# Squares of the residual placed later on ScalarE in the last stage of a hybrid encoder block

## The chip, the cores and the metric

One core of a Trainium2 chip runs the kernel. The metric is device time in microseconds of one execution, from the same chip for the kernel before and after; lower is better. TensorE (PE in the profile) multiplies matrices into PSUM, VectorE (DVE) and ScalarE (ACT) do elementwise work, GpSimd (POOL) does little here but issue DMAs that add to what lies in memory, SyncE (SP) issues the other DMAs. Each engine works through one queue in order, so an operation that waits holds all that stand behind it.

## The reference

256 rows of width 4096, everything in float32. After a norm, one wide product feeds chunked attention and a convolution module; their gated results go through `w_out` and are added to `x`. The last stage, which the change is about, is this:

```
h = h + jnp.concatenate([y_a, y_c], axis=-1) @ w_out[i]
gate = jax.nn.sigmoid(rms_norm(h, ple_norm_g[i]) @ w_ple_gate[i] + b_ple_gate[i])
h = h + gate * (p[i] @ w_ple[i])
return rms_norm(h, final_g)
```

So every row needs the sum of squares of the final h over all 4096 columns, and each element is multiplied by `final_g` and by the row's inverse root.

## The kernel before, in words

**Precision and tiling.** A float32 product is made of three matmuls on float32r parts: the high part of the weights `wh` (a cast on ScalarE) and the low part `wl` (weights minus `wh`, a subtraction on VectorE), both in `parts_of`, line 204 and 205. The activations, transposed and split once, lie in SBUF; the weights stream through. A product is made for a pair of column blocks of 512 at a time (`mixed_product`). Its 32 row blocks of 128 form 16 units of two. A *plain* unit is 24 matmuls of 512 columns. A *seven* unit (marked `*`, `+` or `-` in the orders) uses Strassen's seven products and needs 21, for which VectorE first forms four sums of weight blocks, `ua` and `ub` (lines 518 to 532); they are cast and subtracted like weights, as `uh` and `ul`. Units marked `+` have `ua` formed by DMAs that add, and use it only in the products from `w_in`.

**Buffers.** Loaded weights `wt` have five, `wh` and `wl` three each, `uh` and `ul` two, `ua` and `ub` two between them. The seven units' extra products P1, P5, P7, P6 take the four PSUM banks of the pool `ps_tmp`, which the embedding product `pacc` of the column pair before has held. Rows broadcast over partitions (bias of the gate, `final_g`) share three buffers.

**The last stage.** `gated_pair` runs for the column pairs 0, 2 and 4 (pairs 1, 2 and 3 in the text); the last pair has its own code, with the order `final` in place of `dense`. In a gated pair, 16 units of `w_ple_gate` are followed by the embedding product from `w_ple` (line 237). Then, for each quarter of the pair's 256 x 1024 block, the gate is finished on VectorE (line 1269) and put through a sigmoid on ScalarE (line 1270). What is left is not issued at once but put in a list, `later`: the gate times the embedding on VectorE (into `z`, which frees a bank of `pacc`), a DMA on POOL's queue that adds `z` to the residual `hc` (written in line 1272, L184 in the profile), eight empty places, the squares of `hc` with their row sums on ScalarE (line 610, output `junk`), and `hc` times `final_g` on VectorE. Helpers such as `tt` have one line for all their uses, so the profile shows those two multiplies as L184, told apart by their tiles: `z<-acc,z` and `hc<-hc,row`.

**The order.** `mixed_product` of the next pair calls `fill(4)` after each unit, which writes four entries of the list: the multiplies and their DMAs in units 0 and 1, eight empty places in units 2 and 3, the squares in unit 4, the weight multiplies in unit 5, the loads of two bias rows (appended when the first seven unit begins) in unit 6. That is program order only. A planner then orders every engine's queue by simulating the program with its own costs: an operation takes its engine when its inputs are there by that simulation, so one can be issued long before its place in the program if its engine is idle. `tc.issue_after(ins)` gives all that is written within it on `ins`'s engine an edge: they are queued behind `ins`, without a wait.

`recent` holds what `parts_of` made last. Units marked `+` use it (`queued_behind`): the cast and the subtraction of `ua` are queued behind those of the weights before them.

The orders that matter, the number being the pair of row blocks:

```
dense = units("1 0* 3 2* 5 4* 6* 7 8* 9 10* 11 12* 14* 13 15")
final = units("1 0* 3 2* 5 4* 6* 7 8* 9 10* 12* 11 13 14 15")
```

Unit 0 is thus the plain "1", unit 1 the seven "0*", unit 6 "6*".

Of the kernel before, what the change touches and what calls it, by code (L numbers as in the profile page):

```python
# [25 lines left out]
def hybrid_block(  # L26
# [153 lines left out]
    later = deque()  # L180
# [6 lines left out]
    def weight_parts(w, col, k0, kc, tiles=None):  # L187

        wt = wpool.tile([P, KC, NB], F32, tag="w", name="wt")
        nc.sync.dma_start(  # L190
            wt[:, :kc, :],
            w[k0 * P : (k0 + kc) * P, col : col + NB].rearrange("(k q) n -> q k n", q=P),
        )
        return parts_of(wt, kc, tiles)[0]

    def part_tiles():
        return [wpool.tile([P, KC, NB], F32R, tag=tag, name=tag, bufs=3) for tag in ("wh", "wl")]

    def parts_of(wt, kc, tiles=None):
        if tiles is None:  # L200
            tiles = part_tiles()
        wh, wl = tiles
        made = (
            nc.scalar.copy(wh[:, :kc, :], wt[:, :kc, :]),  # L204
            nc.vector.tensor_tensor(  # L205
                wl[:, :kc, :], wt[:, :kc, :], wh[:, :kc, :].bitcast(F32), ALU.subtract
            ),
        )
        recent[:] = made
        return (wh, wl), made  # L210

    def high_and_minus(wt):
# [7 lines left out]
    recent = []  # L220

    @contextmanager
    def queued_behind(made):

        with ExitStack() as queued:
            for ins in made:
                queued.enter_context(tc.issue_after(ins.ins))
            yield

    def accumulate(acc, h, lhs, kb, wh, wl, k, kblocks, then=lambda ins: None):  # L230
        t, i = lhs[kb // 4], kb % 4
        xh = t[:, i, 0, h * P : (h + 1) * P]
        xl = t[:, i, 1, h * P : (h + 1) * P]
        for kind in range(3):
            a, b = ((xh, wh), (xl, wh), (xh, wl))[kind]
            then(
                nc.tensor.matmul(  # L237
                    acc, a, b[:, k, :],
                    start=kb == 0 and kind == 0, stop=kb == kblocks - 1 and kind == 2,
                )  # L240
            )

    def product(w, col, lhs, kblocks, pool=None, tag="acc", fills=2):

        acc = [
            (pool or ps_acc).tile([P, NB], F32, tag=tag, name=f"acc{h}") for h in range(NH)
        ]
        for k0 in range(0, kblocks, KC):
            kc = min(KC, kblocks - k0)
            wh, wl = weight_parts(w, col, k0, kc)  # L250
            for k in range(kc):
                for h in range(NH):
                    accumulate(acc[h], h, lhs, k0 + k, wh, wl, k, kblocks)
            fill(fills)
        return acc
# [79 lines left out]
    def pair_parts(src):  # L335

        tiles = [upool.tile([P, 2, NB], F32R, tag=tag, name=tag) for tag in ("uh", "ul")]
        return parts_of(src, 2, tiles)[0]
# [38 lines left out]
    def mixed_product(  # L377
# [93 lines left out]
        for n, (pair, seven, by_dma) in enumerate(order):  # L471
# [13 lines left out]
            if n >= len(order) - n_left:  # L485
                for k in range(2):
                    tiles = left[2 * (n - len(order) + n_left) + k]
                    held.append((2 * pair + k, parts_of(wts[k], 2, tiles and tiles())[0]))
                fill(fills[n % len(fills)])
                continue  # L490
# [29 lines left out]
            with queued_behind(before if seven == "+" else ()):  # L520
                uah, ual = pair_parts(ua)
# [50 lines left out]
    def helper_sums(helper, z):  # L572


        nc.scalar.copy(z[1][0], helper["P1"])
        tt(z[1][0], helper["P6"], z[1][0], ALU.add)
        tt(z[0][1], helper["P5"], z[1][0], ALU.add)
        tt(z[1][0], helper["P7"], z[1][0], ALU.add)
        tt(z[1][1], helper["P5"], z[1][0], ALU.add)

    def sum_tiles(*homes):

        homes = homes or (dict(tag="stage"),) * 2
        t = [spool.tile([P, NH, NB], F32, name="z", **kw) for kw in homes]
        return t, [[t[j][:, h] for j in range(2)] for h in range(NH)]
# [481 lines left out]
    def broadcast_row(src, n0, n, **kw):  # L1067

        kw = kw or dict(tag="row", bufs=3)
        t = spool.tile([P, n], F32, name="row", **kw)  # L1070
        nc.sync.dma_start(
            t, bass.AP(tensor=src.tensor, offset=src.offset + n0, ap=[[0, P], [1, n]])
        )
        return t
# [122 lines left out]
    for c0 in range(0, D // NB, 2):  # L1197
        for j in range(2):
            hc = act.tile([P, NH, NB], F32, tag="act", name="hc")
# [20 lines left out]
        for h, j in QUARTERS:  # L1220
            hc = hs[c0 + j][:, h, :]
# [10 lines left out]
    ssq_f = cpool.tile([P, NH, n_f + 2], F32, name="ssq_f")  # L1232
    nc.vector.memset(ssq_f[:, :, :1], EPS)
    square_f = partial(square_sum, scale=D ** -0.5)
# [4 lines left out]
    def gated_pair(c0, order, ahead):  # L1239

        z, rows, fgs = [], [], []

        def on_begin():
            later.extend(partial(bias_row, rows, c0 + j) for j in range(2))

        def on_helpers(helper):
            z.extend(sum_tiles()[1])
            stt(z[0][0], helper["P1"], r_h[:, :1], rows[0], ALU.mult, ALU.add)
            helper_sums(helper, z)
            for h, j in QUARTERS[1:]:  # L1250
                zz = z[h][j]
                stt(
                    zz, zz, r_h[:, h : h + 1], rows[j],
                    ALU.mult, ALU.subtract if j else ALU.add,
                )
            fgs.extend(broadcast_row(final_g, (c0 + j) * NB, NB) for j in range(2))

        acc = mixed_product(
            w_ple_gate[0], c0 * NB, hT, hS, order, on_helpers, ahead=ahead, fills=(4,),
            on_begin=on_begin,  # L1260
        )
        pacc = [
            product(w_ple[0], (c0 + j) * NB, pT, PLE // P, pool=ps_tmp, tag="tmp", fills=0)
            for j in range(2)
        ]
        squares, weights = [], []
        for h, j in QUARTERS:
            gt, hc = z[h][j], hs[c0 + j][:, h, :]
            stt(gt, acc[h][j], r_h[:, h : h + 1], gt, ALU.mult, ALU.subtract if j else ALU.add)
            nc.scalar.activation(gt, gt, AF.Sigmoid)  # L1270
            later.append(partial(tt, gt, pacc[j][h], gt, ALU.mult))
            later.append(partial(nc.gpsimd.dma_start, hc, gt, accum_op=ALU.add))
            squares.append(partial(square_f, ssq_f[:, h, 1 + c0 + j : 2 + c0 + j], hc))
            weights.append(partial(tt, hc, hc, fgs[j], ALU.mult))
        later.extend([lambda: None] * 8 + squares + weights)

    for c0 in range(0, n_f - 2, 2):
        gated_pair(c0, dense if c0 else late, None if c0 else h_ahead)


    c0 = n_f - 2
# [100 lines left out]
    squares = []  # L1382
# [45 lines left out]
```

## Time and profile before

| | |
|---|---|
| median of 3 runs | 2049.0 us (2047.79 to 2050.46) |
| the profiled execution | 2048.76 us |
| its span, first to last instruction | 2047.0 us |
| TensorE busy | 98% |
| VectorE busy | 94% |
| ScalarE busy | 61% |
| granted TensorE clock, mean | 0.998 |
| the last stage, with the products of `w_ple_gate` | from about 1650 us on |

The profile shows one execution. Its span leaves out 1.76 us at the ends. A timeline row gives start, length, engine, line, operation, what it writes and reads, and in brackets how long the engine had been idle and what ended that. A matmul's length overlaps with that of the next, so the pace is read from a stretch: its time by its matmuls. A table by stretches gives the span of each, then busy time and instructions of PE, weight loads (PEld), DVE, ACT and POOL, the granted clock, the DMA share and GB/s.

### The profile page before, as it was taken

Reading aid. Unit: us, or ns where it says so; the run is one execution under the profiler, and the core shown is the slowest. Engines: PE = TensorE matmul, PEld = TensorE weight load, DVE = VectorE, ACT = ScalarE, POOL = GpSimd, SP = SyncE. Lnnn points to the kernel's source line nnn. Section 1 sums busy time; section 2 is a strip of 40 time slices with the busy share of each in tenths; the row PEclk is TensorE's granted clock in tenths of the full one; section 3 lists DMA queues with packets and bytes.
Section 4 is the critical chain, followed back from the end, with each engine's and each line's share of the span. In section 5 each row is a group of like instructions: output and inputs, shape, how many; then the busy total and the mean of one; then the engine's idle time right before and its main releaser. Section 6 shows DMA issues by size and latency. Waiting matters only on the chain. (4 is left out here: it accounts for less than half of the span.)

```text
span 2047.0 us, 26349 instructions
## 1 busy us (share of the span) xinstructions
PE 2009.9 (98%) x9043; PEld 1648.4 (81%) x9043; DVE 1922.0 (94%) x2759; ACT 1258.1 (61%) x1634; POOL 75.8 (4%) x83
## 2 busy tenths in 40 slices
PE   9999999999999999999999999999999999898987
PEld 7888888878888888888888788888888888686866
DVE  7999999889999998989999999999999999898997
ACT  7655455664656556775666566766676665555554
POOL 0000000000000000000000000000000000000000
PEclk9999999999999999999999999999999999999999
DMA  8787878679678877556678677776876856766665
GB/s 288 224 238 233 257 212 251 176 229 256 183 214 256 242 211 224 179 177 205 211 218 250 202 236 222 223 248 201 237 227 219 246 172 222 206 217 206 216 209 170
DMA packets 175921, 450.86 MB, mean 220 GB/s; under 512 B 14494, under 2 KB 17710, under 8 KB 175786
## 3 DMA queue, kind: packets, MB, share of 16 engines
q1 hardware_dynamic: 161952, 417.93, 63.5%
q0 software_dynamic: 13184, 30.41, 8.7%
q8 instruction: 71, 1.16, 0.2%
q10 hardware_dynamic: 650, 0.84, 0.1%
q14 instruction: 64, 0.52, 0.1%
HBM read 441.78 MB, written 4.19 MB: 218 GB/s over the span
## 5 line engine op out<-in xcount | busy, mean ns | idle before, releaser
L420 PE MATMUL acc<-wh,big_t 128*128 128x512 f32 x4028 | 1240.7, 391 | 1.6 <-DVE z L1138 1.6
L204 ACT CAST wh<-wt 128x1024 fp32r<-128x1024 f32 (+1 forms) x716 | 684.1, 965 | 480.8 <-PE acc L420 349.1
L420 PEld LDWEIGHTS acc<-wh,big_t 128*128 128x128 f32 x4028 | 753.6, 188 | 158.0 <-issue 1.7
L205 DVE TENSOR_TENSOR wl<-wt,wh 128x1024 fp32r<-128x1024 f32 (+1 forms) x716 | 791.6, 1117 | 43.2 <-ACT wh L204 37.1
L420 PE MATMUL acc<-wl,big_t 128*128 128x512 f32 x1958 | 759.9, 392 | 0.1
L420 PEld LDWEIGHTS acc<-wl,big_t 128*128 128x128 f32 x1958 | 367.4, 188 | 77.2 <-DVE wl L205 1.2
L204 ACT CAST uh<-ua 128x1024 fp32r<-128x1024 f32 x187 | 196.5, 1051 | 101.8 <-DVE ua L519 50.0
L205 DVE TENSOR_TENSOR ul<-ua,uh 128x1024 fp32r<-128x1024 f32 x187 | 228.9, 1224 | 13.1 <-ACT uh L204 10.3
L787 DVE SCALAR_TENSOR_TENSOR cv<-uT,dw,cv 128x255 f32<-128x255 f32 (+23 forms) x480 | 206.8, 478 | 1.1
L420 PE MATMUL acc_P<-uh,big_t 128*128 128x512 f32 x570 | 176.7, 392 | 11.8 <-DVE z L184 6.9
L420 PEld LDWEIGHTS acc_P<-uh,big_t 128*128 128x128 f32 x570 | 105.7, 188 | 38.7 <-DVE z L184 8.1
L204 ACT CAST uh<-ub 128x1024 fp32r<-128x1024 f32 x99 | 104.1, 1052 | 50.1 <-DVE ub L532 41.1
L205 DVE TENSOR_TENSOR ul<-ub,uh 128x1024 fp32r<-128x1024 f32 x99 | 120.8, 1221 | 3.5 <-ACT uh L204 3.1
L420 PE MATMUL acc_P<-ul,big_t 128*128 128x512 f32 x285 | 111.5, 393 | 7.0 <-DVE ul L205 7.0
L518 DVE TENSOR_TENSOR ua<-wt 128x512 f32<-128x512 f32 x112 | 77.0, 687 | 14.6 <-DMA wt<-in_w_in_dram 8.7
L420 PE MATMUL acc<-uh,big_t 128*128 128x512 f32 x286 | 88.3, 389 | 0.0
L420 PE MATMUL acc_P<-wh,big_t 128*128 128x512 f32 x286 | 88.2, 389 | 0.0
L519 DVE TENSOR_TENSOR ua<-wt 128x512 f32<-128x512 f32 x112 | 76.9, 687 | 3.8 <-DMA wt<-in_w_in_dram 3.0
L420 PEld LDWEIGHTS acc_P<-ul,big_t 128*128 128x128 f32 x285 | 53.3, 188 | 22.3 <-DVE ul L205 11.3
L420 PE MATMUL acc_P<-uh,comb_t 128*128 128x512 f32 x228 | 70.2, 390 | 0.3 <-ACT uh L204 0.3
L532 DVE TENSOR_TENSOR ub<-ub,wt 128x512 f32<-128x512 f32 x99 | 68.2, 689 | 1.6
L531 DVE TENSOR_TENSOR ub<-ua,wt 128x512 f32<-128x512 f32 x99 | 67.9, 686 | 0.0
(254 smaller groups left out, 1637.7 us busy)
## 6 DMA issues: line engine op xcount, KB each, us to landing
wt<-in_w_in_dram SPq DMA_DIRECT2D x416, 512.0 KB, 4.7
wt<-in_w_out_dram SPq DMA_DIRECT2D x128, 512.0 KB, 4.5
wt<-in_w_ple_gate_dram SPq DMA_DIRECT2D x128, 512.0 KB, 4.2
wt<-in_w_pw_dram SPq DMA_DIRECT2D x32, 512.0 KB, 4.5
ua<-in_w_in_dram SPq DMA_DIRECT2D x31, 512.0 KB, 4.6
ua<-in_w_in_dram POOLq DMA_DIRECT2D x31, 512.0 KB, 8.5
wt<-in_w_in_dram SPq DMA_DIRECT2D x31, 256.0 KB, 2.7
low<-in_w_in_dram POOLq DMA_DIRECT2D x12, 512.0 KB, 8.8
```

Source lines behind the costliest of these rows:

```text
L204: nc.scalar.copy(wh[:, :kc, :], wt[:, :kc, :]),
L205: nc.vector.tensor_tensor(wl[:, :kc, :], wt[:, :kc, :], wh[:, :kc, :].bitcast(F32), ALU.subtract),
L420: nc.tensor.matmul(banks[name], a, b, start=name not in begun, stop=final and ends[name] == n and kind == 2 and not (left and name in "P2 ...
L518: plus(ua[:, 0], w0[:, 0], w0[:, 1])
L519: plus(ua[:, 1], w0[:, 1], w1[:, 1])
L531: plus(ub[:, 0], ua[:, 0], w1[:, 1])
L532: plus(ub[:, 1], ub[:, 0], w1[:, 0])
L787: nc.vector.scalar_tensor_tensor(cv[:, i, PAD - k :], uT[:, i, : T + k - PAD], dw[:, b, k : k + 1], cv[:, i, PAD - k :], ALU.mult, ALU.add,)
```

## The change

The squares of a gated pair are written eight empty places later: sixteen in place of eight, so in unit 6 of the next product, the weight multiplies in unit 7 and the bias rows in unit 8. And each square is queued on ScalarE behind the cast that `parts_of` wrote last before it. For that, `recent` keeps the cast alone (`made[:1]`) in place of cast and subtraction, in all products.

```
         recent[:] = made
+        recent[:] = made[:1]
         return (wh, wl), made
...
+    recent = []
+
+    def behind_cast(work, *args):
+
+        with tc.issue_after(recent[0].ins):
+            return work(*args)
...
-            squares.append(partial(square_f, ssq_f[:, h, 1 + c0 + j : 2 + c0 + j], hc))
+            squares.append(partial(behind_cast, square_f, ssq_f[:, h, 1 + c0 + j : 2 + c0 + j], hc))
             weights.append(partial(tt, hc, hc, fgs[j], ALU.mult))
-        later.extend([lambda: None] * 8 + squares + weights)
+        later.extend([lambda: None] * 16 + squares + weights)
```

The second `recent = []` binds the same name anew before anything uses it. `gated_pair` runs three times; the squares of its last run fall into the last pair's product.

## The prediction

> **What bounds the kernel now.** I read the page's busy times first, then a table of busy time by stretch, then the waits of the last stage, then its timeline engine by engine.
>
> ```profile
> span 2047.0 us, 26349 instructions
> PE 2009.9 (98%) x9043; PEld 1648.4 (81%) x9043; DVE 1922.0 (94%) x2759; ACT 1258.1 (61%) x1634; POOL 75.8 (4%) x83
> ```
>
> TensorE is busy nearly all the time and VectorE close behind, so a change pays only where one of the two stands still. The stretches below give span, then busy time and instruction count of PE, weight loads, DVE, ACT and POOL. The first three begin about where the gate product of pairs 2, 3 and 4 of column blocks takes over, the last two lie inside pair 2.
>
> ```profile
> 1746.50:1840.90 94.40, 88.57 (x385) 71.28 (x384) 85.44 (x103) 53.11 (x64) 3.56 (x4) 1.00 0.70 212
> 1840.90:1937.20 96.30, 89.15 (x386) 71.47 (x385) 85.44 (x103) 52.53 (x63) 3.46 (x4) 1.00 0.67 208
> 1937.20:2012.00 74.80, 69.30 (x297) 54.70 (x296) 67.53 (x81) 42.76 (x52) 3.47 (x4) 1.00 0.71 211
> ...
> 1746.50:1785.00 38.50, 32.67 (x139) 25.46 (x138) 31.55 (x40) 20.80 (x29) 3.56 (x4) 1.00 0.74 205
> 1785.00:1830.00 45.00, 45.00 (x199) 36.79 (x198) 44.25 (x52) 26.02 (x28) 0.00 (x0) 1.00 0.69 221
> ```
>
> From 1785 to 1830 us TensorE never stops: 45.00 us for 199 matmuls is 0.2261 us a matmul, the pace I use below. Pair 2 has 385 matmuls, 87.1 us at that pace, and takes 94.40: 7.3 us are lost, all before 1785. Pair 3 loses 96.30 - 386 x 0.2261 = 9.0 us, the last product up to 2012 loses 74.80 - 297 x 0.2261 = 7.6 us. Together 24.0 us: the most this change can win. In the waits of the last stage (total, times, longest) the squares head a chain through three engines:
>
> ```profile
> ACT junk L610 <- DMA hc<-z: 31.2, 12, 5.4
> DVE wl L205 <- ACT wh L204: 12.8, 5, 3.5
> DVE ul L205 <- ACT uh L204: 10.5, 6, 3.3
> PE acc_P L420 <- DVE z L184: 6.9, 3, 2.7
> PE acc_P L420 <- DVE ul L205: 6.6, 6, 1.7
> ```
>
> All twelve squares that wait are those of pairs 1 to 3. They stand in ScalarE's queue in front of casts of weights whose data is there, and wait for the accumulating DMA into hc. How that reaches TensorE is seen in pair 2 (ACT, DVE, PE rows; the bracket is the idle time before):
>
> ```profile
> 1747.67 1.05 ACT L204 CAST uh<-ua 128x1024 fp32r<-128x1024 f32 x1
> 1750.76 0.63 ACT L610 ACTIVATE junk<-hc 128x512 bf16<-128x512 f32 x1 [2.04 <-DMA hc<-z]
> 1751.29 0.19 ACT L610 ACTIVATION_READ_ACCUMULATOR junk<-hc 128x1 f32 x1
> ...
> 1753.81 1.03 ACT L204 CAST wh<-wt 128x1024 fp32r<-128x1024 f32 x1
> ...
> 1765.58 0.63 ACT L610 ACTIVATE junk<-hc 128x512 bf16<-128x512 f32 x1 [2.89 <-DMA hc<-z]
> 1766.21 1.03 ACT L204 CAST uh<-ua 128x1024 fp32r<-128x1024 f32 x1
> ...
> 1750.71 0.68 DVE L532 TENSOR_TENSOR ub<-ub,wt 128x512 f32<-128x512 f32 x1
> 1754.87 1.22 DVE L205 TENSOR_TENSOR wl<-wt,wh 128x1024 fp32r<-128x1024 f32 x1 [3.47 <-ACT wh L204]
> 1756.01 0.68 DVE L184 TENSOR_TENSOR z<-acc,z 128x512 f32<-128x512 f32 x1
> ...
> 1747.13 0.61 PE L420 MATMUL acc<-wh,big_t 128*128 128x512 f32 x2
> ...
> 1753.70 0.39 PE L420 MATMUL acc_P<-ul,big_t 128*128 128x512 f32 x1
> 1756.75 0.73 PE L420 MATMUL acc_P<-uh,big_t 128*128 128x512 f32 x2 [2.66 <-DVE z L184]
> ...
> 1767.29 0.73 PE L420 MATMUL acc_P<-uh,big_t 128*128 128x512 f32 x2 [0.73 <-ACT uh L204]
> 1768.56 0.50 PE L420 MATMUL acc_P<-ul,big_t 128*128 128x512 f32 x1 [0.53 <-DVE ul L205]
> 1771.38 0.73 PE L420 MATMUL acc_P<-uh,big_t 128*128 128x512 f32 x2 [0.26 <-ACT uh L204]
> 1773.77 0.50 PE L420 MATMUL acc_P<-ul,big_t 128*128 128x512 f32 x1 [1.66 <-DVE ul L205]
> ```
>
> The second cast of unit 1 (1753.81) sits behind two squares, the subtraction of it (1754.87) behind the cast, the third gate multiply (1756.01) behind the subtraction, and only that multiply frees the PSUM bank in which helper P7 begins. The last four lines are the second half: the cast for unit 3 stands behind the fourth square, and VectorE, having idled, cannot catch up within the unit.
>
> **The change, part by part.** (1) *The squares leave the head of ScalarE's queue.* Until pair 2's unit 6 nothing else holds the casts. The cast at 1753.81 needs a wh buffer that TensorE frees with the 12th matmul of unit 0, 1747.13 + 12 x 0.2261 = 1749.84, when ScalarE has been free since 1748.72. So it ends near 1750.9, the subtraction follows the VectorE operation that ends at 1751.39 and takes 1.22, the third multiply 0.68: 1753.3. TensorE is ready for P7 one matmul after the row of 1753.70, at 1753.93. Stall one is gone, with 0.6 us to spare. The cast at 1766.21 likewise no longer waits for 1765.58, and VectorE comes to unit 3 some 4 us earlier, more than the 1.66 us and its small companions.
>
> (2) *Where the squares go.* Sixteen empty places at four a unit fill units 2 to 5, so they are written after unit 6 ("6*") and queued behind its last cast, that of ub. Unit 6 starts 135 matmuls (three plain units of 24, three of 21) after unit 0: 1747.13 + 30.5 = 1777.7 unstalled, 1785.0 in the trace; the difference is again the 7.3 us.
>
> ```profile
> 1788.55 1.05 ACT L204 CAST uh<-ub 128x1024 fp32r<-128x1024 f32 x1
> 1792.53 1.06 ACT L204 CAST wh<-wt 128x1024 fp32r<-128x1024 f32 x1 [2.93 <-issue]
> ...
> 1759.08 0.86 POOL L184 DMA_DIRECT2D hc<-z  x1 [0.87 <-PE acc L420]
> ...
> DMA to landing us min/median/max: 2.0/3.9/8.3
> ```
>
> Here is that cast, and ScalarE idles 2.93 us right behind it. Four squares at 0.72 us from start to next start (the first ends its read of the sum at 1751.48, 0.72 after its start) are 2.9 us: they fit in the hole, price nothing. Without the hole the next weights' cast would be up to 2.9 us late. Their data: the fourth DMA, issued even now 12 us into the product (1759.08), lands 8.3 us later at the worst, by 20; the squares come from 34 us on. The wait is gone, not moved. POOL's queue gains nothing to wait for; its DMAs start earlier, with the multiplies.
>
> (3) *The four weight multiplies hc x final_g* (L184) must follow the squares and are written in unit 7 instead of 5. Four of 0.69 us (the row below), 2.8 us of VectorE, go from a stretch where it stands idle into one where it is busy 44.25 of 45.00. In the old place they cost nothing; in the new, between nothing (VectorE arrives ahead by what it no longer loses) and 2.8 us a pair. I take 0.5, because of the second row:
>
> ```profile
> L184 DVE TENSOR_TENSOR hc<-hc,row x12: 684/689/693, 1765.1 to 1971.8; 128x512 f32<-128x512 f32 x12
> ...
> 1786.46 1.23 DVE L205 TENSOR_TENSOR ul<-ua,uh 128x1024 fp32r<-128x1024 f32 x1
> ```
>
> VectorE now begins unit 6's first sum 1.5 us after TensorE begins the unit. Unhindered, the buffer for it comes free 12 matmuls before the unit starts (2.7 us), and after a cast of 1.05 it begins 1.7 us before: some 3 us further ahead than now, when this lag still gave no stall.
>
> (4) *Bias rows* are written in unit 8 instead of 6 and take a row buffer that the weight multiplies free.
>
> ```profile
> SPq L1071 <- DVE hc L184: 10.2, 6, 2.0
> DVE ua L518 <- DMA wt<-in_w_ple_gate_dram: 4.0, 3, 1.4
> ...
> wt<-in_w_ple_gate_dram SPq DMA_DIRECT2D x94, 512.0 KB, 4.1
> ```
>
> SP already stands up to 2.0 us for them, and weight loads stand behind. The wait moves with the multiplies; the rows would land some 42 us into the product and are needed after its last seven-product unit, not before 60 (267 matmuls in the last product, 312 in the others). Nothing, with 0 to 2 us as bounds.
>
> (5) *The list of the latest cast now holds the cast alone.* The 31 units of the input projections whose sums come by DMA used it to hold two operations back, the cast of ua on ScalarE and its subtraction on VectorE. The first stays. The second loses its edge, but needs a cast that comes behind the cast the older subtraction needs; the older is ready first. Nothing; the other end is rival E.
>
> ```profile
> ua<-in_w_in_dram POOLq DMA_DIRECT2D x31, 512.0 KB, 8.5
> ...
> PE acc_P L420 <- ACT uh L204: 2.0, 3, 1.5
> ```
>
> **The sum.** By TensorE, 24.0 us. By VectorE: its waits for casts, 12.8 + 10.5 us, are the squares' doing but for one in the tail:
>
> ```profile
> 2018.06 1.23 DVE L205 TENSOR_TENSOR ul<-wt,uh 128x1024 fp32r<-128x1024 f32 x1 [0.85 <-ACT uh L204]
> ```
>
> That leaves 22.4 us. VectorE can't turn all of it into lead: only two uh and three wh buffers let it run ahead, so in units 4 to 6 it will wait for TensorE to free them, by my count about 1 us a pair, and with 0.5 from (3) that is 1.5 for each of three: 22.4 - 4.5 = 18. Between 18 and 22.4 I take 20. The profiled execution took 2048.76 us (1.76 beside its span), 0.24 under the median of the runs shown: 2048.76 - 20 = 2028.8, and with those 0.24, 2029.
>
> **The rivals.**
> *A, the forecast*: gain 16 to 24, 2025 to 2033.
> *B, VectorE becomes the bound.* For it: 85.44 us of work a pair against 87.1 of TensorE's leaves 1.6 us, and the multiplies move into the fuller half. If the second half of the stalls (0.73, 0.53, 0.26 and 1.66 of idle in pair 2, about 3 each time) stays and the multiplies cost their 2.8 each, the gain is 24.0 - 9 - 8.4 = 6.6; with the stalls alone 15. That is 2034 to 2042, say 2038. Against it: 45 us at 98% VectorE without a stall. [...]
> *C, no effect.* The squares could land where they still wait, or another wait (the gate multiplies behind some other subtraction) hold the P7 bank as long. The DMA's 14 us of lead at the new place speaks against it. 2049.
> *D, slower by SP.* If the row load keeps its place among the weight loads while the multiplies move two units (24 + 21 matmuls, 10.2 us), SP stands 10.2 + 2.0 = 12.2 us. Weights have five buffers, about 2.5 us of TensorE each, less a load's 4.1 and the casts: some 5 us of cover. So 7 us lost per pair at the first row load, and perhaps 4 at final_g's, 33 in all against 24: 2058. It turns into a loss once SP stands more than about 13 us a pair. Against it: the order of SP's queue is planned from the same release, which moves too.
> *E, slower by the lost edge.* If in the input projections the subtraction for ua (1.22 us) overtakes the older one, that one is 1.22 us late; with no cover at all 31 x 1.22 = 38 us, 2067, and a loss from 17 of the 31 on. Against it: the older is ready first, and between 60 and 930 us TensorE's waits in these groups are the 2.0 us of the row in (5) and little else. A handful of them would only trim A.
>
> **How the numbers follow.** A 0.68, B 0.18, C 0.05, D 0.05, E 0.04. Faster by over 0.2% (4 us; less can't be told from no change here): A, B and 0.01 of C, 0.87; within 0.2%: the rest of C and 0.01 of E, 0.05; slower: D and the rest of E, 0.08. The time is A's. The range reaches over A and most of B: 2024.5 to 2042; A's own is 2025 to 2033.
>
> **What would show it.** Right: no wait of junk for hc's DMA left in the three stretches (31.2 us now); waits of wl and ul for casts down from 23.3 to a few us; the third gate multiply some 6 us after its product starts, not 8.9; pair periods of 88 to 89 us in place of 94.4 and 96.3; squares behind the cast of ub in unit 6, in what was ACT's idle time. B would show as acc_P waiting for ul in units 7 to 12; D as a long SP wait at L1071 and ua waiting for wt; E as TensorE waits before 930 us. The forecast is wrong if TensorE's period stays above 91 us though the squares no longer wait.

## The result and the profile after

The changed kernel takes 2023.32 us in the median (2023.0 to 2024.9, four runs) against 2048.72 for the kernel before on the same chip (2047.79 to 2050.46, four runs): the ratio is 0.9877, with a 95% interval of 0.9859 to 0.9894. That is 25.4 us, more than the 20 forecast, and 1.2 us below the low end of the range. A second comparison, on another occasion, gave 0.9894 (0.9880 to 0.9907), 22.9 us.

The profiled execution took 2023.59 us, its span is 2021.8. First the page's busy times, then the stretches of the last stage, cut as before from one first accumulating DMA to the next (span, then busy time and instructions of PE, PEld, DVE, ACT, POOL).

```profile
PE 2003.7 (99%) x9043; PEld 1650.4 (82%) x9043; DVE 1920.5 (95%) x2759; ACT 1259.6 (62%) x1634; POOL 75.8 (4%) x83
```

```profile
1744.09:1831.75 87.66, 87.66 (x389) 72.58 (x388) 85.10 (x103) 54.10 (x64) 3.56 (x4) 1.00 0.73 228
1831.75:1918.44 86.69, 86.69 (x384) 71.80 (x383) 85.04 (x103) 52.91 (x63) 3.46 (x4) 1.00 0.74 231
1918.44:1986.80 68.36, 68.12 (x300) 55.70 (x298) 67.05 (x81) 43.56 (x52) 3.47 (x4) 1.00 0.75 232
```

TensorE is busy all through pairs 2 and 3: 87.66 us for 389 matmuls is 0.2253 us each. From the first matmul of pair 2 to that of pair 3 it takes 1831.94 - 1744.90 = 87.0 us, against 1841.70 - 1747.13 = 94.6 before. VectorE's work is nearly the same (237.2 us in the three stretches, 238.4 before), its idle time is not: 94.40 - 85.44, 96.30 - 85.44 and 74.80 - 67.53 made 27.1 us before, 2.6 + 1.7 + 1.3 make 5.5 now. The waits of the last stage show what is left: in the stretches VectorE waits for weights from memory and, once, 1.1 us for a cast of activations (`big_t`); the wait for uh lies in the tail. SP's stand at the bias rows is half of what it was.

```profile
DVE ua L526 <- DMA wt<-in_w_ple_gate_dram: 4.5, 4, 1.7
DVE big_t L205 <- ACT big_t L204: 1.1, 1, 1.1
...
DVE ul L205 <- ACT uh L204: 0.7, 1, 0.7
```

```profile
SPq L1079 <- DVE hc L184: 5.2, 6, 0.9
```

No `junk <- DMA hc<-z` is left; it was 31.2 us. In the timeline of pair 2 (ACT rows, DVE rows, PE row; lines from 229 on moved by eight) the second weight cast of unit 1 no longer stands behind a square, the third gate multiply follows the subtraction of it, and the squares stand behind the cast of ub in unit 6 at 1775.47:

```profile
1747.64 1.05 ACT L204 CAST wh<-wt 128x1024 fp32r<-128x1024 f32 x1 [1.15 <-issue]
...
1775.47 1.06 ACT L204 CAST uh<-ub 128x1024 fp32r<-128x1024 f32 x1 [0.30 <-PE acc L428]
1776.43 0.62 ACT L618 ACTIVATE junk<-hc 128x512 bf16<-128x512 f32 x1
1776.96 0.19 ACT L618 ACTIVATION_READ_ACCUMULATOR junk<-hc 128x1 f32 x1
1777.05 1.04 ACT L204 CAST wh<-wt 128x1024 fp32r<-128x1024 f32 x1
1778.00 0.62 ACT L618 ACTIVATE junk<-hc 128x512 bf16<-128x512 f32 x1
...
1748.88 1.22 DVE L205 TENSOR_TENSOR wl<-wt,wh 128x1024 fp32r<-128x1024 f32 x1
1750.01 0.69 DVE L184 TENSOR_TENSOR z<-acc,z 128x512 f32<-128x512 f32 x1
...
1779.55 2.49 DVE L184 TENSOR_TENSOR hc<-hc,row 128x512 f32<-128x512 f32 x4
...
1744.90 0.62 PE L428 MATMUL acc<-wh,big_t 128*128 128x512 f32 x2
```

The third multiply ends 5.8 us after the product's first matmul (1750.70 - 1744.90), 9.6 before (1756.69 - 1747.13). The four weight multiplies run as one block of 2.49 us.

From the first accumulating DMA of pair 2 to the end of the span it was 2047.0 - 1746.53 = 300.5 us and is 2021.8 - 1744.09 = 277.7: 22.8 us come from the stage that the change touches. The remaining 2.4 us lie before it. There the two programs do not differ: up to the first of these squares, every engine's planned order and the waits written into it are the same in both kernels.

### The profile page after: what moved, and what is told of

Same layout as the page of the kernel before. It is cut to its first block, busy times and chain, and to the rows that moved or that the text cites. A ratio compares the mean times of both kernels' runs of the same rounds, so it can differ in the third digit from the quotient of the medians.

```text
span 2021.8 us, 26364 instructions
## 1 busy us (share of the span) xinstructions
PE 2003.7 (99%) x9043; PEld 1650.4 (82%) x9043; DVE 1920.5 (95%) x2759; ACT 1259.6 (62%) x1634; POOL 75.8 (4%) x83
## 4 chain that ended last, share of the span: by engine, by line
PE 93%; DVE 3%; DMA 2%; issue 2%; ACT 1%; POOLq 0%; POOL 0%; ACTq 0%; DVEq 0%
PE acc L428 70%; PE acc_P L428 18%; PE tmp_ps L170 1%; DVE wl L205 1%; PE acc L245 1%; DMA wt<-in_w_in_dram 1%; DVE cv L795 1%; DMA low<-in_w_in_dram 0%; DVE ul L205 0%; PE tmp_ps L967 0%; PE tmp_ps L951 0%; PE tmp_ps L985 0%; PE tmp_ps L990 0%; DMA wt<-in_w_ple_dram 0%; DMA wt<-in_w_ple_gate_dram 0%
## 5 line engine op out<-in xcount | busy, mean ns | idle before, releaser
L526 DVE TENSOR_TENSOR ua<-wt 128x512 f32<-128x512 f32 x112 | 76.7, 685 | 12.6 <-DMA wt<-in_w_in_dram 6.3
```

The costliest lines, as they stand in the source:

```text
L526: plus(ua[:, 0], w0[:, 0], w0[:, 1])
```

## The experiments

All times below are medians, with the ratio to the kernel before on the same occasion (2046.3, 2046.8 and 2045.6 us). "Stage" is the time from the first accumulating DMA of pair 2 to the end of the span in that run's profile; it leaves out the part before, in which the start of that DMA wanders between 1742.0 and 1746.5 us.

| run | median us | ratio, 95% interval | stage us |
|---|---|---|---|
| kernel before | 2048.7 in the first comparison | | 300.5 |
| edge_only | 2048.2 | 1.0010 (1.0001 to 1.0019) | 302.7 |
| places_only | 2047.0 | 1.0007 (0.9998 to 1.0017) | 300.2 |
| places_0 | 2040.1 | 0.9968 (0.9955 to 0.9981) | 294.1 |
| last_two_behind | 2036.5 | 0.9953 (0.9938 to 0.9967) | 290.9 |
| squares_of_z | 2027.5 | 0.9904 (0.9887 to 0.9921) | 279.5 |
| no_weights | 2023.9 | 0.9890 (0.9876 to 0.9905) | 276.2 |
| after_again | 2023.4 | 0.9894 (0.9880 to 0.9907) | 278.7 |
| behind_only | 2023.1 | 0.9894 (0.9881 to 0.9908) | 278.6 |
| places_24 | 2022.9 | 0.9892 (0.9874 to 0.9909) | 277.0 |
| places_4 | 2022.2 | 0.9888 (0.9872 to 0.9903) | 277.4 |

**The lost edge alone, and the change once more.** The edit is against the kernel before; the second run has none, it is the changed kernel again.

```
         recent[:] = made
+        recent[:] = made[:1]
```

> The kernel before with one edit: the list of the latest cast holds the cast alone. Theory 1 (all of the gain comes from the squares): every engine's planned order and waits are those of the kernel before, so 2048 to 2050 us, and the first accumulating DMA of pair 2 starts at 1744 to 1748 us, which shows how far that moment wanders by itself. Rival (the lost edge gave the 2.4 us by which that DMA started earlier): 2046 us and a start near 1744.

> The changed kernel once more, as a second sample. Theory 1: 2023 to 2025 us, 277 to 279 us from the first accumulating DMA of pair 2 to the end (300.5 in the profile before), and that DMA anywhere between 1744 and 1748. Rival: that DMA at 1744 again, since the 2.4 us belong to the change.

With the edit of the list alone, the planned order and the waits of all five engines are those of the kernel before: it is the same program, but for line numbers. It took 2048.2 us where the kernel before took 2046.3, and its first accumulating DMA of pair 2 started 1.9 us earlier than in the first profile. The changed kernel's second profile has that DMA at another moment too, 0.85 us earlier than the 1744 to 1748 expected (in this order: the changed kernel's first profile, edge_only, the changed kernel's second profile; in the kernel before it started at 1746.53):

```profile
1744.09 1.83 POOL L184 DMA_DIRECT2D hc<-z  x2 [88.38 <-DVE z L184]
```

```profile
1744.61 1.83 POOL L184 DMA_DIRECT2D hc<-z  x2 [88.10 <-DVE z L184]
```

```profile
1743.15 1.83 POOL L184 DMA_DIRECT2D hc<-z  x2 [88.09 <-DVE z L184]
```

So the 2.4 us ahead of the stage are not the lost edge, whose program does not differ; two loads of one program lie 1 to 2 us apart, for a reason that no run here shows. What the change itself is worth is better read from the stage, 22.8 us in the first pair of profiles, and from the second comparison, 22.9. The stage wanders too: 302.7 us in edge_only against 300.5 for the same program, 278.7 against 277.7 for the changed kernel, so by these four profiles the gain lies between 21.8 and 25.0.

**Each half of the edit alone.** The first against the kernel before, the second against the changed kernel.

```
-        later.extend([lambda: None] * 8 + squares + weights)
+        later.extend([lambda: None] * 16 + squares + weights)
```

> The kernel before with sixteen empty places but no queueing behind the cast. Theory 1 (the planner pulls a square forward to where its own simulation has the data ready, so the place in the program means little): squares stay in front of the casts of units 1 to 3 and wait for the DMA some 30 us in all, 2044 to 2050 us. Rival (the later place alone does it): no waits, 2024 us.

```
-        later.extend([lambda: None] * 16 + squares + weights)
+        later.extend([lambda: None] * 8 + squares + weights)
```

> The changed kernel with eight empty places as before: squares queued behind the last cast of unit 4, some 20 us into the product, when the DMAs have landed if they start at 0 to 9 us as in the changed kernel and take up to 8.3. Theory 1: no or nearly no wait for hc, 2023 to 2027 us, the sixteen places add little. Rival (the distance of sixteen places is needed): squares wait 5 us or more in all, 2030 us or more.

The later place without the queueing does nothing: the squares are pulled forward to the same spot of ScalarE's queue, and the waits of places_only are nearly those of before:

```profile
ACT junk L610 <- DMA hc<-z: 27.9, 12, 4.0
DVE wl L205 <- ACT wh L204: 14.1, 9, 2.9
DVE ul L205 <- ACT uh L204: 8.7, 6, 2.5
```

The queueing without the later place does all of it: no wait for hc, 2023.1 us. The eight extra places are worth nothing that these runs can tell.

**How far behind.** No empty places, four, and twenty-four, with the queueing (against the changed kernel, in the same line: `[lambda: None] * 16 +` left out, then `* 4`, `* 24` in place of `* 16`).

> The changed kernel with no empty places: squares queued behind the last cast of unit 2, some 10 us into the product, when the third and fourth DMA, issued at 7 and 9 us, have mostly not landed. Theory 1 (what counts is whether the data is there when the queue comes to the square): some 5 to 20 us of waits for hc, 2025 to 2038 us. Rival (the queueing alone is enough, wherever): no waits, 2023 us.

> The changed kernel with four empty places: squares queued behind the last cast of unit 3, some 14 to 17 us into the product. With no empty places the fourth DMA landed 17 us in, with eight nothing waited. Theory 1 (only the landing counts, and the last one comes 13 to 17 us in): waits for hc of 0 to 3 us in all, 2023 to 2028 us. Rival (each unit of distance is worth its share, on the line from 2040 at none to 2023 at eight): near 2031 us.

> The changed kernel with twenty-four empty places: squares in unit 8, multiplies by final_g in unit 9, bias rows in unit 10. Theory 1 (once the data is there, the place does not matter, and VectorE has room for the multiplies anywhere): 2022 to 2025 us. Rival (VectorE's load in the later units, 98% busy, or the row loads behind the multiplies now cost something): 2027 us or more.

Without empty places, in unit 2, the first two squares find their data and the last two don't (ACT rows of places_0, pair 2; in pair 3 the second square waits 0.7 us as well):

```profile
1753.83 0.63 ACT L618 ACTIVATE junk<-hc 128x512 bf16<-128x512 f32 x1
...
1758.16 0.63 ACT L618 ACTIVATE junk<-hc 128x512 bf16<-128x512 f32 x1 [2.85 <-DMA hc<-z]
...
1762.56 0.63 ACT L618 ACTIVATE junk<-hc 128x512 bf16<-128x512 f32 x1 [3.16 <-DMA hc<-z]
1763.09 0.18 ACT L618 ACTIVATION_READ_ACCUMULATOR junk<-hc 128x1 f32 x1
1763.19 1.03 ACT L204 CAST uh<-ua 128x1024 fp32r<-128x1024 f32 x1
```

That alone keeps some 16 us of the loss, 2040.1 us where 2025 to 2038 were expected. One unit later nothing waits and the time is that of the changed kernel (2022.2, 0.8 under the 2023 to 2028 expected); at twenty-four places it still is. It is a step, not a slope: the rival's 2031 us for four places are not there. The last square can start 16 us into the product (1762.56 - 1746.47, the first matmul's start in that run), and anything from unit 3 on is late enough here.

**The same place without the DMA.** Against the kernel before.

```
-            squares.append(partial(square_f, ssq_f[:, h, 1 + c0 + j : 2 + c0 + j], hc))
+            squares.append(partial(square_f, ssq_f[:, h, 1 + c0 + j : 2 + c0 + j], gt))
```

> The kernel before, but the early squares of pairs 1 to 3 read the gated embedding z instead of the residual hc, so that they stand in the same place of ScalarE's queue and wait for no DMA. Left out: the right row sums, so the output is not the reference's. Theory 1 (the wait for the DMA holds the casts): the 31 us of waits vanish and most of the gain is there, 2022 to 2030 us. Rival (four squares of 0.72 us in front of casts are themselves too much at that place): TensorE still waits several us in each stretch, 2036 us or more.

With squares as early as before or one or two casts earlier, but of data that is there, 2027.5 us: the 2.9 us of ScalarE's own work are not the harm. TensorE's waits in the stage fall to this one row:

```profile
PE acc_P L420 <- DVE ul L205: 1.5, 3, 0.6
```

Of the 4 us above the changed kernel, only 0.8 to 1.8 lie in the stage (279.5 us against 278.7 and 277.7), where that row has 1.5. The rest lies ahead of it: the first accumulating DMA started at 1746.2 us in this profile, at 1744.1 and 1743.2 in those of the changed kernel.

**The two halves of the stall.** Against the changed kernel.

```
-            squares.append(partial(behind_cast, square_f, ssq_f[:, h, 1 + c0 + j : 2 + c0 + j], hc))
+            square = partial(square_f, ssq_f[:, h, 1 + c0 + j : 2 + c0 + j], hc)
+            squares.append(partial(behind_cast, square) if j == 1 else square)
```

> The changed kernel with only the third and fourth square of a pair queued behind the cast; the first two go where the planner puts them, as before. Theory 1 (two halves: squares one and two make the P7 stall, three and four the stalls of unit 3): the wait for P7's bank stays, 2 to 3 us a pair with its restart, those of unit 3 go; 2028 to 2038 us, squares wait some 8 to 12 us in all. Rival (the second half is the echo of the first, through VectorE's delay): both stay, 2040 us or more; or neither, if the first two alone do no harm: 2024 us.

With only the first two squares early, the wait for P7's bank stays whole, and part of what I had put down to the second half stays with it (TensorE's waits in the stage; before, the three were 6.9, 6.6 and 2.1, with 2.7 for uh):

```profile
PE acc_P L428 <- DVE z L184: 6.7, 3, 3.0
PE acc_P L428 <- DVE ul L205: 3.6, 3, 1.3
PE acc_P L428 <- ACT wh L204: 0.8, 2, 0.4
```

So neither story is whole. Each run's gain over the kernel before on its own occasion gives an estimate: of the 22.9 us of the change, last_two_behind has 10.3 (2046.8 - 2036.5) and places_0 6.7 (2046.8 - 2040.1). Squares one and two then cost 12.6 us, three and four 16.2 (places_0, where but for 0.7 us only they wait), and both together 22.9, so some 6 us are shared. (A little of the 16.2 is slower matmuls: in places_0 the granted clock was 0.98 in the stretch of pair 2, from 1735 to 1835 us, and 0.97 in that of pair 4, from 1930 to 1980; it was 1.00 in the same stretches of last_two_behind.) That VectorE's delay from the first stall is still there when the second would come would explain it; no run shows this.

**VectorE with less to do.** Against the changed kernel; VectorE's busy time falls from 1920.5 to 1914.4 us.

```
-        later.extend([lambda: None] * 16 + squares + weights)
+        later.extend([lambda: None] * 16 + squares + [lambda: None] * 4)
```

> The changed kernel without the twelve multiplies of hc by final_g in pairs 1 to 3. Left out: that factor in 6 of the 8 column blocks, so the output is not the reference's. 7.2 us of VectorE's work are gone. Theory 1 (TensorE sets the pace in the changed kernel, VectorE has room and the multiplies in their new place cost nothing): 2021 to 2025 us, as with them. Rival (VectorE is the bound, and the multiplies cost up to 2.8 us a pair): 2015 to 2020 us.

2023.9 us: nothing is won by taking the twelve multiplies away. In the stretch of the profile that holds pair 2, TensorE never stops, without them (first row) or with them (the changed kernel, second row):

```profile
1735.00:1835.00 100.00, 100.00 (x443) 82.83 (x442) 95.29 (x114) 61.45 (x74) 4.69 (x6) 1.00 0.73 227
1735.00:1835.00 100.00, 100.00 (x443) 82.81 (x442) 96.22 (x118) 61.74 (x75) 5.29 (x6) 1.00 0.73 228
```

TensorE sets the pace of the changed kernel in this stage up to the tail, and the multiplies are free where they now stand, as far as the times can tell. The stage of this one profile, 276.2 us, is 1.5 to 2.5 us shorter than in the changed kernel's two; as TensorE stood idle for only 0.24 us of the three stretches of the first of these, no wait for the multiplies there explains that.

## Why the prediction was right and wrong

- **The chain** (squares, casts, subtractions, gate multiplies, P7's bank) was right: squares_of_z takes the DMA out of it and 19 of the 23 us are there; last_two_behind leaves its head and the P7 stall is back.
- **Step (1)**, the third multiply done 6.2 us into the product: 5.8 measured. (The 8.9 that the prediction sets beside it is where that multiply started before; it ended at 9.6.) The stalls of unit 3 went as well.
- **Step (2)**, the place and the cover: right. The squares stand behind the cast of ub in unit 6 and cost nothing that shows. The row of landings it quotes holds the stores of the output too; the accumulating DMAs alone took 3.9 to 8.3 us, so the worst case stands. Sixteen places, which I took as part of the cure, are not: eight or four do as well, and none of it works without the queueing.
- **Step (3)**, 0.5 us a pair for the multiplies in a stretch 98% full: nothing that the times of no_weights show.
- **Step (4)**: SP's wait at the bias rows went from 10.2 to 5.2 us, and no wait of TensorE came of it.
- **Step (5)**, the lost edge: nothing, shown by edge_only, the same program.
- **The sum** is the step that failed. From VectorE's 22.4 us of waits I took off 4.5: 1 a pair for waits on full buffers in units 4 to 6, and 0.5 a pair for (3). No row of VectorE's waits names a buffer there. Its idle time in the three stretches came to 5.5 us; with the 4.5 it should have been 27.1 - 22.4 + 4.5 = 9.2, without it 4.7. So at most 0.8 of the 4.5 exists. The stage gained 22.8 us: 21.6 of idle time and 1.2 by which VectorE's busy time in the stretches came out shorter. The estimate by TensorE was the nearer one: pair 2 takes 87.0 us from first matmul to first matmul where I had counted 87.1 unstalled, and the periods that I expected at 88 to 89 us came to 87.7 and 86.7. The planner, free of the early squares, also put VectorE's work in another order, which I had not tried to follow.
- **The range** went wrong by a second thing: its low end, 2024.5, is the whole 24.0 off the median of the kernel before and half a us more, with no room for what two loads of a program differ by. The kernel before took 2048.7, 2046.3, 2046.8 and 2045.6 us on its four occasions, so the first, from which the time was forecast, was the slowest. With 1 to 2 us for that, 2023.3 lies inside. The 2.4 us ahead of the stage, without which the result would have been near 2025.7, are not the work of the change.
- **The rivals**: B (VectorE as the bound) is refuted by no_weights: 2023.9 us, where 2015 to 2020 were to be expected of it. In the stretch from 1735 to 1835 us TensorE, at 82.8% of weight loads, had no room left with the multiplies or without (busy 100.00 of 100.00 us, 443 matmuls, one every 0.226 us), and VectorE, at 95 to 96%, made it wait nowhere. C is what places_only is. D and E did not happen.

## What to carry to other kernels

An operation that waits for a slow transfer (here an accumulating DMA of 3.9 to 8.3 us) belongs behind the work that its engine could do meanwhile; where a planner orders the queue by its own idea of the transfer, a later place in the program does not put it there (places_only, 2047.0 us), an order edge does (behind_only, 2023.1 us). Find out when the data lands and queue it just behind that: one unit too early kept some 16 of 23 us of the loss here, later gained nothing. And where the waits removed were nearly the only ones, take the whole of them: a discount for a bound needs its own row. Leave room in a range for what two loads of the same program differ by, here 1 to 2 us.

## What the runs showed of the hardware

Some of the kernel-before's stalls cost more than their length: behind one of 1.66 us matmuls took 0.425 us each, 0.23 a little later. In the first profile the granted clock stayed at 1.00 in the three stretches. In edge_only, the same program, it fell to 0.96, 0.96 and 0.95 in the three stretches, and the stage took 302.7 us in place of 300.5; the slices show it at 0.79 where a stall lies (pair 2):

```profile
1744.00:1752.00 8.00, 8.00 (x37) 6.63 (x36) 5.47 (x8) 4.49 (x8) 1.83 (x2) 1.00 0.91 226
1752.00:1760.00 8.00, 5.56 (x18) 4.13 (x17) 5.83 (x6) 4.27 (x7) 1.73 (x2) 0.79 0.62 159
```

The timeline of that run shows the slower matmuls behind the idle time of 1.66 us:

```profile
1771.99 0.67 PE L421 MATMUL acc_P<-ul,big_t 128*128 128x512 f32 x1 [1.66 <-DVE ul L205]
1772.45 1.05 PE L421 MATMUL acc<-uh,big_t 128*128 128x512 f32 x2
1773.30 0.63 PE L421 MATMUL acc<-ul,big_t 128*128 128x512 f32 x1
...
1776.42 0.39 PE L421 MATMUL acc<-wl,big_t 128*128 128x512 f32 x1
1776.65 0.61 PE L421 MATMUL acc<-wh,big_t 128*128 128x512 f32 x2
```

From 1772.45 to 1773.30 two matmuls take 0.425 us each, three microseconds later it is 0.23 again. In last_two_behind an idle time of 2.98 us was followed by the full pace, 0.23 us a matmul from 1754.20 on:

```profile
1753.63 0.73 PE L428 MATMUL acc_P<-uh,big_t 128*128 128x512 f32 x2 [2.98 <-DVE z L184]
1754.20 0.40 PE L428 MATMUL acc_P<-ul,big_t 128*128 128x512 f32 x1
1754.43 0.62 PE L428 MATMUL acc<-wh,big_t 128*128 128x512 f32 x2
1754.89 0.39 PE L428 MATMUL acc<-wl,big_t 128*128 128x512 f32 x1
```

So the length of one idle time alone does not decide it; what does was not tried. The changed kernel, without such stalls, keeps 1.00 in all three stretches.
